# Feed-forward LayerNorm: ScalarE normalises, scale and shift are applied per partition behind the transpose

## The chip, the cores and the metric

One core of one Trainium2 chip runs the kernel as a single launch. The metric is the device time of that launch in microseconds (us), the median of several runs. All times of this document come from runs of these kernels and from one profiled execution of each.

## What is computed

A decoder trunk of two post-norm residual layers on one sequence of 256 tokens with 2048 channels, all in float32. What matters here is the LayerNorm that stands between a layer's mixer and its feed-forward part:

```python
for layer in range(2):
    mix = even_mixer(...) if layer % 2 == 0 else odd_mixer(...)
    x = layer_norm(ALPHA * x + mix, mix_ln_g[layer], mix_ln_b[layer])
    hid = jnp.square(jax.nn.relu(x @ ffn_w1[layer]))            # 2048 -> 8192
    x = layer_norm(ALPHA * x + hid @ ffn_w2[layer], ffn_ln_g[layer], ffn_ln_b[layer])

def layer_norm(x, g, b):       # mean and variance over the 2048 channels of a token
    return (x - mean) * rsqrt(var + EPS) * g + b
```

## The kernel before

The residual `xres` lies with tokens on partitions: two token blocks `tb` of 128 tokens, each with 2048 channels, handled in four chunks `n` of 512. A matrix product needs the activations the other way round, channels on partitions. So a normalised chunk goes through TensorE as four 128x128 transposes into one PSUM tile `tp` (`transpose4`, L219), of which there are two in turn. ScalarE then copies `tp` into the high part `actAh` (L213), and VectorE writes the rest, `tp` minus the high part, into `actAl` (L214). Weights are split in the same way, `wh` by ScalarE (L191) and `wl` by VectorE (L192). Every product is three matmuls: high by high, high by the weight's rest, the rest by high (L870 to L872).

The program is a list of units. A unit is six matmuls: one weight tile of two 128-channel blocks, for one token block. `at(u, f)` hangs a task in front of unit u, and the tasks of a unit are issued in the order in which they were hung, each onto its engine. Every engine runs its own instructions strictly in that order and waits on counters that the other engines raise; the framework puts in the waits.

Around a LayerNorm the units are ordered so that token block 0 ends six units ahead of token block 1, and the next stage starts with token block 0. With the last product of a token block, `z_add` adds the accumulator to `xres` and takes statistics (`bns`), `ln_stats` makes mean and reciprocal deviation (ScalarE's square root `lnsd`, L558, then three small VectorE operations ending in `lny`), `ln_apply` normalises a chunk on VectorE in two operations (L573: minus mean, times `gB`; L578: times `lny`, plus `bB`), and `ln_t` transposes and splits it. `gB` and `bB` hold scale and shift copied to all 128 partitions. In the stretch of a LayerNorm, weights are not split ahead (`hold`), unless a tile is due within four units: two are, in the second half.

Four LayerNorms are made so: ahead of the feed-forward part of layer 0 (unit group `F0u00`, about 333 us) and of layer 1 (`F1u00`, about 1441 us), ahead of layer 1's mixer (`Dk0`, about 1051 us), and, without transposes, at the end. The change is to the first two. Behind them the first product of the feed-forward part goes through `relu2` (ScalarE: relu of `acc` into `rl`, L608, then its square, L609) and is transposed four units after that product's end (`relu2_t`, rows named `tp<-ident,rl`).

Of the kernel before, what the change touches and what calls it, by code (L numbers as in the profile page):

```python
# [10 lines left out]
FT = mybir.dt.float32  # L11
# [18 lines left out]
SKEW = 6  # L30
HOLD = 4
LAND, EACH, FIRST = 3, 1.3, -1
FILL = 352
MAGIC = float(0x5F3759DF - 0x00400000)

LAG = dict(gl=7, eq=4, ek=5,
# [32 lines left out]
def trunk_kernel(ctx, tc, a, out):  # L69
# [71 lines left out]
    def at(u, f, *args):  # L141
        tasks.setdefault(u, []).append((f, args))
# [369 lines left out]

    at(start["EO00"] + 6, open_res)

    def open_ffn(g, b, u):
        st = ExitStack()
        p = st.enter_context(tc.tile_pool(name="ffnp", bufs=1, side="left"))
        fstack["s"], fstack["p"] = st, p
        load_gb(g, b, u)

    def load_gb(g, b, u):
        p = fstack["p"]
        box["g"] = p.tile([128, D], FT, name="gB")
        box["b"] = p.tile([128, D], FT, name="bB")
        for n in range(4):
            for k, (name, t) in enumerate(((g, box["g"]), (b, box["b"]))):
                src = a[name]
                at(u + 4 * n + 2 * k, SY.dma_start, t[:, n * 512:(n + 1) * 512],
                   bass.AP(tensor=src.tensor, offset=src.offset + n * 512, ap=[[0, 128], [1, 512]]))

    def conv_close():
        cstack.close()
        open_extra()
        open_ffn("mg0", "mb0", conv_done + 1)

    at(conv_done + 1, conv_close)

# [42 lines left out]
    def ln_t(tb, n):  # L580
        tp = transpose4(res["x"][:, tb, n * 512:(n + 1) * 512])
        to_act("A", slice(4 * n, 4 * n + 4), tp.rearrange("p (c t) -> p c t", t=128),
               slice(tb * 128, (tb + 1) * 128))

    def ln_out(tb, n):
        SY.dma_start(out[tb * 128:(tb + 1) * 128, n * 512:(n + 1) * 512], res["x"][:, tb, n * 512:(n + 1) * 512])

    def layer_norm(tb, u, nxt, final=False):
        at(u + 1, ln_stats, tb)
        if final:  # L590
            at(u + 2, ln_gain, tb, 0)
            for n in range(4):
                if n < 3:
                    at(u + 2, ln_gain, tb, n + 1)
                at(u + 2, ln_shift, tb, n)
                at(u + 2, ln_out, tb, n)
            return
        if tb == 0:
            at(u - 1, warm, AF.Sqrt)
            hold.update(range(u, when[nxt, 6, 1]))  # L600
        for n in range(4):
            need = when[nxt, 2 * n, tb]
            at(u + 1 + n, ln_apply, tb, n)
            at(max(u + 2 + n, min(u + 4 + 2 * n, need - 1)), ln_t, tb, n)

    def relu2(acc, tb):
        r = fstack["p"].tile([128, 512], FT, name="rl", bufs=3)
# [226 lines left out]
    def close_odd():  # L834
        odd["s"].close()
        open_extra()
        open_ffn("mg1", "mb1", start["DO0"] + 6)

    at(start["DO0"] + 6, close_odd)
    for n in range(4):  # L840
# [130 lines left out]
```

## Time and profile before

| what | value |
|---|---|
| median of 3 runs | 2177.4 us (2175.76 to 2177.59) |
| the profiled execution's own time | 2176.42 us |
| its span, first to last instruction | 2174.6 us |
| TensorE (PE) busy | 2154.5 us, 99% of the span |
| VectorE (DVE) busy | 1273.2 us, 59% |
| ScalarE (ACT) busy | 1009.6 us, 46% |
| mean granted TensorE clock | 0.998 of full |

The share of busy time is a mean over the whole program. What a change in one stage is worth is read from that stage: which engine waits there, and for what.

### The profile page before, as it was taken

To read this page: it belongs to the slowest core of one execution; us is meant where nothing else is said; L and a number is where in the kernel's file an instruction comes from. 1 tells how busy PE (TensorE), PEld (TensorE's weight loads), DVE (VectorE), ACT (ScalarE), POOL (GpSimd) and SP (SyncE) were. 2 spreads that over 40 slices of the span, in tenths; PEclk is the share of its full clock that TensorE was granted. 3 is DMA by queue.
4 is the path that set the end of the run, shared out by engine and by line. 5 is a ranking of instruction groups with operands and counts; after the bars stand their busy time and mean duration, and the time that the engine had idled before them with its cause. 6 is when DMAs were issued, how large, how long until landed. Compare 5 with 4: busy or idle time off the path is not lost.

```text
span 2174.6 us, 25528 instructions
## 1 busy us (share of the span) xinstructions
PE 2154.5 (99%) x9742; PEld 1775.7 (82%) x9742; DVE 1273.2 (59%) x1586; ACT 1009.6 (46%) x1184; POOL 0.2 (0%) x4
## 2 busy tenths in 40 slices
PE   8999999999999999999999999999999999999997
PEld 7888887888888888888887888888888888888886
DVE  6998787654445454445656456666554454454454
ACT  5445554643543543453354444436434434534541
POOL 0000000000000000000000000000000000000000
PEclk9999999999999999999999999999999999999999
DMA  7755574756555555555365545737556555555551
GB/s 256 223 193 170 184 255 140 257 187 227 189 192 194 186 187 194 190 183 194 96 202 174 185 157 192 265 102 254 193 193 228 187 193 189 182 195 189 186 191 59
DMA packets 118651, 413.83 MB, mean 190 GB/s; under 512 B 13181, under 2 KB 14973, under 8 KB 118529
## 3 DMA queue, kind: packets, MB, share of 16 engines
q1 hardware_dynamic: 118528, 412.20, 57.8%
q8 instruction: 76, 1.25, 0.2%
q14 instruction: 47, 0.38, 0.0%
HBM read 410.05 MB, written 2.10 MB: 190 GB/s over the span
## 4 chain that ended last, share of the span: by engine, by line
PE 91%; DVE 5%; ACT 1%; DMA 1%; issue 1%; SPq 0%; DVEq 0%; ACTq 0%
PE acc L870 29%; PE acc L872 29%; PE acc L871 29%; PE tp L219 2%; DVE wl L192 1%; DVE xres L573 1%; DVE xres L578 1%; ACT wh L191 1%; DMA raw<-in_w 0%; DVE actAl L214 0%; DMA raw<-in_we_out 0%; DVE bns L549 0%; DVE xres L543 0%; DMA raw<-in_we_in 0%; DVE cv L335 0%
## 5 line engine op out<-in xcount | busy, mean ns | idle before, releaser
L192 DVE TENSOR_TENSOR wl<-raw,wh 128x1024 fp32r<-128x1024 f32 (+1 forms) x753 | 918.0, 1222 | 801.9 <-ACT wh L191 800.9
L191 ACT ACTIVATE wh<-raw 128x1024 fp32r<-128x1024 f32 (+1 forms) x753 | 794.5, 1058 | 907.5 <-PE acc L872 811.2
L870 PE MATMUL acc<-wh,actAh 128*128 128x512 f32 x1728 | 688.3, 398 | 5.8 <-ACT wh L191 5.8
L872 PE MATMUL acc<-wh,actAl 128*128 128x512 f32 x1728 | 675.5, 391 | 0.0
L871 PE MATMUL acc<-wl,actAh 128*128 128x512 f32 x1728 | 674.7, 390 | 0.0
L870 PE MATMUL acc<-wh,actBh 128*128 128x512 f32 x1280 | 501.3, 392 | 0.0
L872 PE MATMUL acc<-wh,actBl 128*128 128x512 f32 x1280 | 498.4, 389 | 0.0
L871 PE MATMUL acc<-wl,actBh 128*128 128x512 f32 x1280 | 498.1, 389 | 0.0
L870 PEld LDWEIGHTS acc<-wh,actAh 128*128 128x128 f32 x1728 | 325.3, 188 | 72.7 <-ACT wh L191 6.5
L872 PEld LDWEIGHTS acc<-wh,actAl 128*128 128x128 f32 x1728 | 324.8, 188 | 68.8
L871 PEld LDWEIGHTS acc<-wl,actAh 128*128 128x128 f32 x1728 | 325.3, 188 | 67.3 <-issue 1.9
L872 PEld LDWEIGHTS acc<-wh,actBl 128*128 128x128 f32 x1280 | 240.2, 188 | 50.4
L871 PEld LDWEIGHTS acc<-wl,actBh 128*128 128x128 f32 x1280 | 240.4, 188 | 49.2
L870 PEld LDWEIGHTS acc<-wh,actBh 128*128 128x128 f32 x1280 | 240.3, 188 | 48.7
L335 DVE SCALAR_TENSOR_TENSOR cv<-hT,cpar,cv 128x256 f32<-128x256 f32 x240 | 102.0, 474 | 0.0
L213 ACT ACTIVATE actBh<-tp 128x512 fp32r<-128x512 f32 x72 | 43.1, 599 | 44.9 <-PE tp L219 44.9
L214 DVE TENSOR_TENSOR actBl<-tp,actBh 128x512 fp32r<-128x512 f32 x72 | 49.5, 688 | 15.1 <-ACT actBh L213 15.1
L545 DVE TENSOR_TENSOR xres<-xres,acc 128x512 f32<-128x512 f32 x56 | 36.7, 680 | 25.4 <-PE acc L872 25.4
L608 ACT ACTIVATE rl<-acc 128x512 f32<-128x512 f32 x64 | 38.2, 597 | 14.2 <-PE acc L872 11.6
L609 ACT ACTIVATE rl<-rl 128x512 f32<-128x512 f32 x64 | 40.5, 632 | 2.0
L219 PEld LDWEIGHTS tp<-ident,rl 128*128 128x128 f32 x256 | 32.0, 141 | 8.3
L219 PE MATMUL tp<-ident,rl 128*128 128x128 f32 x256 | 38.4, 272 | 0.0
(153 smaller groups left out, 482.5 us busy)
## 6 DMA issues: line engine op xcount, KB each, us to landing
raw<-in_w SPq DMA_DIRECT2D x512, 512.0 KB, 3.5
raw<-in_wo_in SPq DMA_DIRECT2D x96, 512.0 KB, 3.5
raw<-in_we_in SPq DMA_DIRECT2D x79, 512.0 KB, 3.6
raw<-in_we_out SPq DMA_DIRECT2D x32, 512.0 KB, 3.7
raw<-in_wo_out SPq DMA_DIRECT2D x32, 512.0 KB, 4.3
xres<-in_xres SPq DMA_DIRECT2D x8, 256.0 KB, 6.1
gB<-in_mg SPq DMA_DIRECT2D x8, 256.0 KB, 6.0
bB<-in_mb SPq DMA_DIRECT2D x8, 256.0 KB, 6.7
```

The source lines that it names most:

```text
L191: A.activation(h[:, c], r[:, c], AF.Copy)
L192: V.tensor_tensor(l[:, c], r[:, c], h.bitcast(FT)[:, c], op=OP.subtract)
L213: A.activation(h[:, kt, cols], tp, AF.Copy)
L214: V.tensor_tensor(l[:, kt, cols], tp, h.bitcast(FT)[:, kt, cols], op=OP.subtract)
L219: PE.transpose(tp[:, i * 128:(i + 1) * 128], src[:, i * 128:(i + 1) * 128], ident)
L335: V.scalar_tensor_tensor(cv[:, ct, :], hT[:, ct, k:k + T], w, cv[:, ct, :], op0=OP.mult, op1=OP.add)
L545: V.tensor_tensor(c, c, acc, op=OP.add)
L608: A.activation(r, acc, AF.Relu)
L609: A.activation(r, r, AF.Square)
L870: PE.matmul(acc, h[:, kt, c], wh[:, w], start=s0, stop=False)
L871: PE.matmul(acc, h[:, kt, c], wl[:, w], start=False, stop=False)
L872: PE.matmul(acc, l[:, kt, c], wh[:, w], start=False, stop=s1)
```

## The change

`ln_apply` and `ln_t` stay for the LayerNorm ahead of `Dk0`. Ahead of the feed-forward parts three functions take their place. `ln_norm` normalises a chunk on ScalarE in one operation, without scale and shift: its scale is `lny` and its bias is `lnm`, which one more small VectorE operation in `ln_stats` makes as minus mean times `lny`. `ln_norm_t` transposes the chunk and applies scale and shift behind the transpose, where a channel is a partition and so its scale and shift are one number per partition (`gbc`, loaded by one more DMA). Since a `tp` tile holds four blocks of channels, that is four ScalarE operations of 128 columns into `actAh` and four VectorE operations of 128 columns into a new tile `yt`, and then one subtraction into `actAl`. `ln_residual` brings scale and shift into `xres` later, with two VectorE operations for each chunk, from unit 44 of the feed-forward part on. `FILL`, a tile that nothing uses, shrinks by as much as the new small tiles take, so that what lies behind it stays where it was.

```diff
-FILL = 352
+FILL = 288
...
+        if cols:
+            box["gc"] = stat.tile([128, 2, KT], FT, name="gbc", bufs=1)
+            at(u, SY.dma_start, box["gc"], a[cols])
...
+        m = stat.tile([128, 1], FT, name="lnm")
+        V.scalar_tensor_tensor(m, mv[:, 0:1], -1.0, y, op0=OP.mult, op1=OP.mult)
+        box["shift", tb] = m
...
+    def ln_norm(tb, n):
+        c = res["x"][:, tb, n * 512:(n + 1) * 512]
+        A.activation(c, c, AF.Identity, scale=box["rstd", tb], bias=box["shift", tb])
+
+    def ln_norm_t(tb, n):
+
+        tp = transpose4(res["x"][:, tb, n * 512:(n + 1) * 512])
+        h, l = act["A"]
+        k, cols, gc = slice(4 * n, 4 * n + 4), slice(tb * 128, (tb + 1) * 128), box["gc"]
+        y = fstack["p"].tile([128, 4, 128], FT, name="yt")
+        for i in range(4):
+            s = tp[:, i * 128:(i + 1) * 128]
+            A.activation(h[:, 4 * n + i, cols], s, AF.Identity, scale=gc[:, 0, 4 * n + i:4 * n + i + 1],
+                         bias=gc[:, 1, 4 * n + i:4 * n + i + 1])
+            V.tensor_scalar(y[:, i, :], s, gc[:, 0, 4 * n + i:4 * n + i + 1], gc[:, 1, 4 * n + i:4 * n + i + 1],
+                            op0=OP.mult, op1=OP.add)
+        V.tensor_tensor(l[:, k, cols], y, h.bitcast(FT)[:, k, cols], op=OP.subtract)
+
+    def ln_residual(tb, n):
+
+        s = slice(n * 512, (n + 1) * 512)
+        c = res["x"][:, tb, s]
+        V.tensor_tensor(c, c, box["g"][:, s], op=OP.mult)
+        V.tensor_tensor(c, c, box["b"][:, s], op=OP.add)
...
-            at(u + 1 + n, ln_apply, tb, n)
-            at(max(u + 2 + n, min(u + 4 + 2 * n, need - 1)), ln_t, tb, n)
+            if nxt[0] == "F":
+                at(u + 1 + n, ln_norm, tb, n)
+                at(max(u + 2 + n, min(u + 4 + 2 * n, need - 1)), ln_norm_t, tb, n)
+                at(start[nxt] + 44 + 4 * (4 * tb + n), ln_residual, tb, n)
+            else:
+                at(u + 1 + n, ln_apply, tb, n)
+                at(max(u + 2 + n, min(u + 4 + 2 * n, need - 1)), ln_t, tb, n)
```

In the rows below the words in brackets name the counter that an instruction waits for: that of PE, of DVE or of ACT ("Activation"). ScalarE before, ahead of `F0u00`, from the first token block's square root to the first forced weight split:

```order
L558 ACTIVATE lnsd<-mv,eps 128x1 [waits DVE_49]
L213 ACTIVATE actAh<-tp 128x4x128 [waits PE_49] x2
L558 ACTIVATE lnsd<-mv,eps 128x1 [waits DVE_49]
L213 ACTIVATE actAh<-tp 128x4x128 [waits PE_49] x3
L191 ACTIVATE wh<-raw 128x1024 [waits DMAHW5_49,Activation_49]
```

ScalarE now, from the first square root to the third chunk:

```order
L561 ACTIVATE lnsd<-mv,eps 128x1 [waits DVE_49]
L593 ACTIVATE xres<-xres,lnm,lny 128x512 [waits DVE_49]
L593 ACTIVATE xres<-xres,lnm,lny 128x512 x2
L603 ACTIVATE actAh<-tp,gbc 128x128 [waits PE_49]
L603 ACTIVATE actAh<-tp,gbc 128x128 [waits DVE_49] x3
L593 ACTIVATE xres<-xres,lnm,lny 128x512
L603 ACTIVATE actAh<-tp,gbc 128x128 [waits PE_49]
L603 ACTIVATE actAh<-tp,gbc 128x128 [waits DVE_49] x3
L561 ACTIVATE lnsd<-mv,eps 128x1 [waits DVE_49]
L593 ACTIVATE xres<-xres,lnm,lny 128x512 [waits DVE_49]
L603 ACTIVATE actAh<-tp,gbc 128x128 [waits PE_49]
L603 ACTIVATE actAh<-tp,gbc 128x128 [waits DVE_49] x3
```

Before, a chunk is one ScalarE instruction that waits for PE. Now it is one to normalise, and four behind the transpose, of which the last three each wait for VectorE. The second square root, which stood behind two copies, stands behind two whole chunks.

VectorE before, at the same place, from the first token block's last normalisation to the second block's statistics:

```order
L573 SCALAR_TENSOR_TENSOR xres<-xres,mv,gB 128x512 [waits DMAHW2_49]
L578 SCALAR_TENSOR_TENSOR xres<-xres,lny,bB 128x512 [waits DMAHW4_49,DVE_49]
L545 TENSOR_TENSOR xres<-xres,acc 128x512 [waits PE_49]
L549 BN_STATS bns<-xres 128x6 [waits DVE_49]
L214 TENSOR_TENSOR actAl<-tp,actAh 128x4x128 [waits Activation_49]
L573 SCALAR_TENSOR_TENSOR xres<-xres,mv,gB 128x512 [waits DMAHW6_49]
L578 SCALAR_TENSOR_TENSOR xres<-xres,lny,bB 128x512 [waits DMAHW0_49,DVE_49]
L214 TENSOR_TENSOR actAl<-tp,actAh 128x4x128 [waits Activation_49]
L545 TENSOR_TENSOR xres<-xres,acc 128x512 [waits PE_49]
L549 BN_STATS bns<-xres 128x6 [waits DVE_49]
L557 BN_AGGR mv<-bns 128x2 [waits DVE_49]
```

VectorE now, from the new small operation to the second block's statistics:

```order
L567 SCALAR_TENSOR_TENSOR lnm<-mv,lny 128x1 [waits DVE_49]
L548 TENSOR_TENSOR xres<-xres,acc 128x512 [waits PE_49]
L552 BN_STATS bns<-xres 128x6 [waits DVE_49]
L605 TENSOR_SCALAR yt<-tp,gbc 128x128 [waits Activation_49] x4
L607 TENSOR_TENSOR actAl<-yt,actAh 128x4x128 [waits DVE_49]
L605 TENSOR_SCALAR yt<-tp,gbc 128x128 [waits DVE_49,Activation_49]
L605 TENSOR_SCALAR yt<-tp,gbc 128x128 [waits Activation_49] x3
L607 TENSOR_TENSOR actAl<-yt,actAh 128x4x128 [waits DVE_49]
L548 TENSOR_TENSOR xres<-xres,acc 128x512 [waits PE_49]
L552 BN_STATS bns<-xres 128x6 [waits DVE_49]
L560 BN_AGGR mv<-bns 128x2 [waits DVE_49]
```

The two normalising operations of each chunk are gone from VectorE. In front of each subtraction stand four operations on `tp`, each of which waits for ScalarE. The second block's statistics still stand behind the first two chunks.

## Rows read from the trace of the kernel before

**Rows 1.** The page, busy time by engine, share of the span.

```profile
PE 2154.5 (99%) x9742; PEld 1775.7 (82%) x9742; DVE 1273.2 (59%) x1586; ACT 1009.6 (46%) x1184; POOL 0.2 (0%) x4
```

**Rows 2.** Stretches around both LayerNorms: length, busy us (count) by engine, clock, DMA.

```profile
325.00:365.00 40.00, 37.94 (x183) 30.73 (x182) 32.02 (x51) 13.97 (x21) 0.00 (x0) 1.00 0.36 117
1430.00:1470.00 40.00, 39.77 (x192) 32.32 (x191) 25.92 (x43) 11.88 (x18) 0.00 (x0) 1.00 0.20 65
```

**Rows 3.** Timeline of PE, layer 0, fifth transposes: start, us, [idle before].

```profile
346.85 0.66 PE L219 MATMUL tp<-ident,xres 128*128 128x128 f32 x4 [1.24 <-DVE actAl L214]
```

**Rows 4.** Timeline of PE: layer 1's last transposes, first of `rl`, both layers.

```profile
1460.11 0.60 PE L219 MATMUL tp<-ident,xres 128*128 128x128 f32 x4
1463.32 0.60 PE L219 MATMUL tp<-ident,xres 128*128 128x128 f32 x4
1469.25 0.60 PE L219 MATMUL tp<-ident,rl 128*128 128x128 f32 x4
...
362.75 0.60 PE L219 MATMUL tp<-ident,rl 128*128 128x128 f32 x4
```

**Rows 5.** Timelines of ACT and DVE around the square roots.

```profile
332.90 0.29 ACT L558 ACTIVATE lnsd<-mv,eps 128x1 f32<-128x1 f32 x1 [2.93 <-DVE mv L557]
...
1440.72 0.29 ACT L558 ACTIVATE lnsd<-mv,eps 128x1 f32<-128x1 f32 x1 [7.55 <-DVE mv L557]
1450.31 0.30 ACT L558 ACTIVATE lnsd<-mv,eps 128x1 f32<-128x1 f32 x1 [2.63 <-DVE mv L557]
...
1441.04 0.16 DVE L560 RECIPROCAL lny<-lnsd 128x1 f32<-128x1 f32 x1 [0.17 <-ACT lnsd L558]
1441.57 0.75 DVE L573 SCALAR_TENSOR_TENSOR xres<-xres,mv,gB 128x512 f32<-128x512 f32 x1
1448.57 0.68 DVE L543 SCALAR_TENSOR_TENSOR xres<-xres,acc 128x512 f32<-128x512 f32 x1
```

**Rows 6.** Groups of ACT by shape: count, busy us, mean ns, idle before.

```profile
L191 ACT ACTIVATE wh<-raw 128x1024 fp32r<-128x1024 f32 x751 | 793.3, 1059 | 904.7 <-PE acc L872 811.2 <-DMA raw<-in_w 30.6 <-DVE cv L335 17.6
L469 ACT ACTIVATE PT<-tp 128x128 f32<-128x128 f32 x8 | 2.2, 280 | 0.0
L360 ACT ACTIVATE c<-cv 128x256 f32<-128x256 f32 x8 | 2.9, 418 | 3.9 <-DVE cv L358 3.9
L385 ACT ACTIVATE c<-c,cpar 128x256 f32<-128x256 f32 x8 | 4.7, 591 | 4.1 <-DVE c L380 4.0
L609 ACT ACTIVATE rl<-rl 128x512 f32<-128x512 f32 x64 | 40.5, 632 | 2.0
```

**Rows 7.** Groups of DVE by shape.

```profile
L578 DVE SCALAR_TENSOR_TENSOR xres<-xres,lny,bB 128x512 f32<-128x512 f32 x32 | 23.8, 750 | 0.8
L214 DVE TENSOR_TENSOR actAl<-tp,actAh 128x512 fp32r<-128x512 f32 x24 | 16.2, 684 | 6.8 <-ACT actAh L213 6.8
L452 DVE CUSTOM_DVE_ANT_0 P<-sd,bias 128x128 f32<-128x128 f32 x8 | 2.3, 287 | 0.9 <-DMA bias<-in_abias 0.8
L332 DVE TENSOR_SCALAR cv<-hT,cpar 128x256 f32<-128x256 f32 x8 | 2.9, 402 | 0.0
L229 DVE TENSOR_SCALAR cyi<-cnh 128x256 int32<-128x256 int32 x1 | 0.3, 294 | 0.0
L192 DVE TENSOR_TENSOR wl<-raw,wh 128x1024 fp32r<-128x1024 f32 x751 | 916.6, 1224 | 799.0 <-ACT wh L191 797.9
```

**Rows 8.** Timeline of ACT in layer 1's mixer: two operations with one pointer operand.

```profile
1117.25 0.51 ACT L715 ACTIVATE wd<-wd,aT 128x256 f32<-128x256 f32 x1 [1.67 <-DVE wd L714]
1117.67 0.39 ACT L716 ACTIVATE wd<-wd,aT 128x128 f32<-128x128 f32 x1
```

**Rows 9.** Clock behind the last matmul (windows); two matmuls at the start (timeline).

```profile
2163.40:2168.00 4.60, 0.00 (x0) 0.00 (x0) 4.25 (x11) 0.29 (x1) 0.00 (x0) 0.78 0.31 114
...
9.46 0.63 PE L870 MATMUL acc<-wh,actAh 128*128 128x512 f32 x1
9.88 0.63 PE L871 MATMUL acc<-wl,actAh 128*128 128x512 f32 x1
```

More of the change, by code (lines that the diff above doesn't have):

```diff
@@ L513, in trunk_kernel, with open_ffn @@
     at(start["EO00"] + 6, open_res)
-    def open_ffn(g, b, u):
+    def open_ffn(g, b, u, cols):
         st = ExitStack()
@@ L518, in open_ffn, with load_gb @@
         fstack["s"], fstack["p"] = st, p
-        load_gb(g, b, u)
-    def load_gb(g, b, u):
+        load_gb(g, b, u, cols)
+    def load_gb(g, b, u, cols=None):
         p = fstack["p"]
+        if cols:
+            box["gc"] = stat.tile([128, 2, KT], FT, name="gbc", bufs=1)
+            at(u, SY.dma_start, box["gc"], a[cols])
         box["g"] = p.tile([128, D], FT, name="gB")
@@ L533, in conv_close @@
         open_extra()
-        open_ffn("mg0", "mb0", conv_done + 1)
+        open_ffn("mg0", "mb0", conv_done + 1, "mc0")
     at(conv_done + 1, conv_close)
@@ L836, in close_odd @@
         open_extra()
-        open_ffn("mg1", "mb1", start["DO0"] + 6)
+        open_ffn("mg1", "mb1", start["DO0"] + 6, "mc1")
     at(start["DO0"] + 6, close_odd)
@@ L958 @@
         arr[f"mg{n}"], arr[f"mb{n}"] = i["mix_ln_g"][n], i["mix_ln_b"][n]
+        arr[f"mc{n}"] = np.stack([i["mix_ln_g"][n], i["mix_ln_b"][n]]).reshape(2, KT, 128).transpose(2, 0, 1)
         arr[f"fg{n}"], arr[f"fb{n}"] = i["ffn_ln_g"][n], i["ffn_ln_b"][n]
```

## The prediction

> **What bounds the kernel now.** I read the page's busy times first: TensorE (PE) is busy 99% of the span, so only a stretch in which PE waits can be shortened, and any wait put before it shows at once [rows 1]. Then the stretches around the two LayerNorms that change: in 40 us, PE idles 2.06 us in layer 0 and 0.23 us in layer 1 [rows 2]. That is all the change can gain: 2.3 us. The largest piece, 1.24 us, is the fifth set of transposes, which waits for one of the two `tp` tiles to be read out by VectorE [rows 3]. So how fast ScalarE and VectorE empty `tp` is what PE meets first. PE wants a chunk every 3.21 us there (1460.11 to 1463.32) [rows 4].
>
> The mark by which I measure the stretch is the first transpose of `rl`: it comes behind all eight chunks on ScalarE's queue and then the relu. From the first square root `lnsd` to it are 28.53 us in layer 1 (1440.72 to 1469.25) and 29.85 us in layer 0 (332.90 to 362.75) [rows 4, 5].
>
> **The change part by part.** Call N a chunk's normalisation on ScalarE, and P its readout from `tp`. Removed from VectorE are two operations of 0.75 us for each chunk [rows 7]. Added are these:
>
> *The readout goes step by step.* The order shows that VectorE's k-th operation on `tp` waits for ScalarE, and ScalarE's next one waits for VectorE. All four blocks lie in one PSUM tile, and the two engines take turns on it: a step is one ScalarE operation, a hand-over, one VectorE operation, a hand-over. Nothing of this sequence overlaps.
> - ScalarE, 128 columns from PSUM without a pointer operand: 0.28 us (L469) [rows 6]. Scale and bias are now one number per partition, read by pointer. At 256 columns an operation has 0.418 us without a pointer (L360), 0.51 with one (L715), 0.591 with two (L385) [rows 6, 8]: two cost 0.17. So 0.45.
> - VectorE, 128 columns from PSUM: 0.287 us (L452); two pointers cost 0.402 (L332) less 0.294 (L229), 0.11 [rows 7]. So 0.39: 0.28 is the bound from below; L332's whole 0.40, at twice the columns, is about as much.
> - A hand-over: square root 1440.72 + 0.29 = 1441.01, VectorE's reciprocal at 1441.04: 0.03 [rows 5].
>
> A step is 0.45 + 0.39 + 0.06 = 0.90 us, four are 3.60, and P without the last hand-over is 3.57. Bounds of a step: 0.28 + 0.29 + 0.06 = 0.63 if pointers were free, and 0.59 + 0.40 + 0.06 = 1.05 if 128 columns cost what the 256 of L385 and L332 cost. Where PE's pace leaves 3.21, P takes 3.57, and VectorE's subtraction (0.68, L214 [rows 7]) comes on top.
>
> The Trainium skill, "ScalarE: Activation LUTs", section "What ACT_TABLE_LOAD costs", gives 186 ns plus 0.833 ns per column, and 93 ns for each pointer operand. The rows here say 0.08 to 0.09 a pointer; by the page the operation is an estimated 0.48 us, and the result would be 1.9 us later.
>
> *N on ScalarE.* 512 columns in SBUF have 0.632 us (L609) [rows 6]; with two pointers 0.80. A successor starts 0.09 before the end (L716 at 1117.67, L715 ending 1117.76) [rows 8], so 0.71 apart. One small operation (`lnm`) joins the chain: the first normalisation began 0.85 us after `lnsd` (1441.57) [rows 5]; with the rest of `lny` and `lnm` I take 1.2.
>
> *The walk*, in us from the first `lnsd`:
> 1. N of chunks 0 to 2 from 1.2; ScalarE is free for P0 at 3.3, which ends at 6.9; subtraction, VectorE free at 7.5.
> 2. ScalarE does N3 and begins P1 at 7.1; VectorE joins at 7.6; P1 ends at 10.7, VectorE is free at 11.3.
> 3. Only then comes the second token block's last `z_add`. From it to its `lnsd` 1.74 us passed (1448.57 to 1450.31) [rows 5]: `lnsd` at 13.0, where it stood at 9.6.
> 4. On ScalarE P2 stands behind that `lnsd` and N of the fifth chunk: 13.0 + 1.2 + 0.71 = 15.0; ends at 18.5. The fifth transposes need P2's tile, as they did before, so PE stands until 18.6.
> 5. Two N, then P3 from 19.4 to 23.0; subtraction to 23.6; P4 to 26.7, its subtraction to 27.3.
> 6. A forced weight split (1.06 on ScalarE, L191, then 1.22 on VectorE, L192 [rows 6, 7]) stands ahead of P5, one ahead of P6. VectorE: split to 29.2, P5 and subtraction to 32.9, split to 34.1, P6 and subtraction to 37.8, P7 to 40.9. PE has the fifth's buffer and late weight tiles to wait for again on the way; all of it lies inside.
> 7. ScalarE ends P7 at 40.5, then relu and square, at most 2 x 0.632 [rows 6]: the transposes of `rl` at 41.8.
>
> So the mark moves by 41.8 - 28.5 = 13.3 us in layer 1 and by 41.8 - 29.9 = 11.9 in layer 0. Behind it the stages are the old ones, and PE has nothing to catch up with.
>
> *The rest costs nothing.* `ln_residual` puts 16 VectorE operations of about 0.7 us into a layer's middle, one pair every four units, where VectorE is busy 59% [rows 1]; without that cover it would be 11 us a layer. The first sum that needs `xres` again comes after unit 72, the last pair. `gbc` is one more small DMA on SP's queue, ahead of the first `gB`; in the time until its use at P0, eight loads of 256 KB pass behind it. `gB` and `bB` are needed later than before. `FILL` moves no address.
>
> **Sum.** The profiled execution's own time is 2176.4 us, 1.0 under the median. 2176.4 + 13.3 + 11.9 = 2201.6, so about 2202 us, 1.1% slower. The bounds: a step of 0.63, with N at 0.63, walked in the same way, puts the mark at 33.5, +5.0 and +3.6: 2185. A step of 1.05 adds 8 x 4 x 0.15 = 4.8 to each LayerNorm: 2211.
>
> **The rivals.**
> *Not slower: the readouts lie side by side.* If the waits were always already met, ScalarE would need 0.71 + 4 x 0.36 = 2.15 us a chunk and VectorE 4 x 0.31 + 0.6 = 1.84, both under PE's 3.21 [rows 4]; PE would lose part of its 2.3 us of waits: 2174 to 2176. It decides at a step of about (3.21 - 0.6) / 4 = 0.65. The waits in the order speak against it, since each step's wait is for the instruction just issued on the other engine; only the free-pointer bound of 0.63 comes near, and step 3 stands even then. Chance 4%.
>
> The Trainium skill, "PSUM — Partial Sum Buffer", section "PSUM bank collisions raise a hardware error", has two engines collide on one bank even where both only read, and the compiler put a dependency between them. By that rule the turns can't be left out. No run here shows a collision.
>
> *Pointers cost little on these operations.* Then a step is near 0.63 and the time near 2186. L385 and L332 are other functions at other widths, which is what speaks for it; three ACT rows in line speak against. Chance 13%.
>
> *PE's clock falls in the long waits and costs extra.* PE stands about six us in step 4. At the program's end PE has nothing to do from 2163.4 on, and the granted clock's mean over the next 4.6 us is 0.78: full for some 2.6 us, then half, 1.2 GHz [rows 9]. At the program's start matmuls come 0.42 us apart (9.46 to 9.88) [rows 9]; twelve of them and a chunk's transposes in 3.21 us [rows 4] leave under 0.27 each at full speed, so a slow one loses about 0.2. Between step 4 and the mark PE has under 16 us of work in a stretch of 23, so one fall is hidden; it costs if the clock is still low behind the mark, some 3.5 us a layer if 16 matmuls are slow: 2209. The Trainium skill, "TensorE: Matmul & The Clock Gate", part 1, has the clock halved after idling; the trace agrees at the end, where the mean of 0.78 shows it. Chance 10%.
>
> **How the numbers follow.** Forecast 73%, the three rivals 4, 13 and 10%. The range runs from just above the lower bound to the upper: 2187 to 2212. About 0.2%, 4.4 us, is what a measurement here can tell from no change. Faster needs the first rival and more than its whole gain: 2%. Same: the rest of it and a pointer-free step with less behind it: 5%. Slower: 93%.
>
> **What would show it.** Right: in the timeline ScalarE's and VectorE's 128-column operations alternate, one step every 0.9 us, and VectorE's idle time is put down to ScalarE's line; PE's longest new wait, about 6 us, is at the fifth transposes; the stretch from the first `lnsd` to the transposes of `rl` is near 42 us in both layers; the LayerNorm ahead of `Dk0` and the end are unchanged. Wrong: a step under 0.65 us; a mark that moves by less than 6 us; PE idle elsewhere, as behind late weights after the mark; or a clock at half for many us behind it.

## The result, and the profile after

The changed kernel takes 2209.34 us (median of 4 runs, 2208.18 to 2210.14) where the kernel before took 2177.03 beside it: 1.0147 times as long, 95% interval 1.0135 to 1.0160. The profiled execution has 2209.19 us, a span of 2207.4 and a mean clock of 0.994.

PE has as many instructions as before; its share of the span is one point lower, although its busy time is 10.1 us longer [rows 1]:

```profile
PE 2164.6 (98%) x9742; PEld 1780.2 (81%) x9742; DVE 1299.0 (59%) x1658; ACT 1039.1 (47%) x1248; POOL 0.2 (0%) x4
```

The first chunk behind the transpose, in layer 0. First ScalarE's timeline, then VectorE's (start, us, instruction, idle time before it and what ended it):

```profile
337.15 0.44 ACT L603 ACTIVATE actAh<-tp,gbc 128x128 fp32r<-128x128 f32 x1
338.07 0.46 ACT L603 ACTIVATE actAh<-tp,gbc 128x128 fp32r<-128x128 f32 x1 [0.48 <-DVE yt L605]
339.01 0.46 ACT L603 ACTIVATE actAh<-tp,gbc 128x128 fp32r<-128x128 f32 x1 [0.48 <-DVE yt L605]
```

```profile
337.63 0.41 DVE L605 TENSOR_SCALAR yt<-tp,gbc 128x128 f32<-128x128 f32 x1 [1.32 <-ACT actAh L603]
338.56 0.41 DVE L605 TENSOR_SCALAR yt<-tp,gbc 128x128 f32<-128x128 f32 x1 [0.53 <-ACT actAh L603]
339.50 0.41 DVE L605 TENSOR_SCALAR yt<-tp,gbc 128x128 f32<-128x128 f32 x1 [0.53 <-ACT actAh L603]
```

Read the two together: ScalarE 338.07 to 338.53, VectorE 338.56 to 338.97, ScalarE 339.01. While one works the other stands, and the idle time of each is put down to the other. A step is 339.01 - 338.07 = 0.94 us.

What PE waits for, over the whole program, the three largest groups that the kernel before does not have (total us, times, longest):

```profile
PE tp L219 <- DVE yt L605: 11.9, 4, 5.6
PE tp L219 <- ACT rl L645: 4.8, 2, 2.4
PE acc L908 <- DVE actAl L607: 4.4, 4, 1.7
```

PE's timeline at the fifth transposes [rows 3] and at the mark [rows 4], layer 0 and then layer 1, and ScalarE's first square root of each [rows 5]:

```profile
352.94 1.12 PE L219 MATMUL tp<-ident,xres 128*128 128x128 f32 x4 [5.60 <-DVE yt L605]
376.94 0.66 PE L219 MATMUL tp<-ident,rl 128*128 128x128 f32 x4 [2.38 <-ACT rl L645]
1476.02 1.12 PE L219 MATMUL tp<-ident,xres 128*128 128x128 f32 x4 [5.61 <-DVE yt L605]
1500.02 0.66 PE L219 MATMUL tp<-ident,rl 128*128 128x128 f32 x4 [2.39 <-ACT rl L645]
```

```profile
333.85 0.30 ACT L561 ACTIVATE lnsd<-mv,eps 128x1 f32<-128x1 f32 x1 [2.93 <-DVE mv L560]
1456.92 0.29 ACT L561 ACTIVATE lnsd<-mv,eps 128x1 f32<-128x1 f32 x1 [7.55 <-DVE mv L560]
```

So from `lnsd` to the mark it is 43.09 us in layer 0 and 43.10 in layer 1, 13.24 and 14.57 more than before. From the mark to the next LayerNorm's first `lnsd` it is 689.41 and 689.43 us, where before it was 687.74 both times: 1.67 and 1.69 more. These are the next `lnsd`, before and then after:

```profile
1050.49 0.29 ACT L558 ACTIVATE lnsd<-mv,eps 128x1 f32<-128x1 f32 x1 [8.85 <-DVE mv L557]
2156.99 0.29 ACT L558 ACTIVATE lnsd<-mv,eps 128x1 f32<-128x1 f32 x1 [25.17 <-DVE mv L557]
```

```profile
1066.35 0.30 ACT L561 ACTIVATE lnsd<-mv,eps 128x1 f32<-128x1 f32 x1 [8.85 <-DVE mv L560]
2189.45 0.30 ACT L561 ACTIVATE lnsd<-mv,eps 128x1 f32<-128x1 f32 x1 [25.17 <-DVE mv L560]
```

The remaining 1.63 us of the span's 32.8 lie ahead of layer 0's first `lnsd` (0.95), between `Dk0` and `F1u00` (0.34) and at the end (0.34).

The clock, from the table of stretches (length, busy us and count of PE, PEld, DVE, ACT, POOL, then granted clock and DMA):

```profile
350.00:355.00 5.00, 2.06 (x7) 1.87 (x8) 2.40 (x6) 3.45 (x7) 0.00 (x0) 0.55 0.00 0
375.00:380.00 5.00, 3.06 (x11) 2.55 (x12) 3.17 (x5) 3.13 (x6) 0.00 (x0) 0.78 0.01 3
380.00:385.00 5.00, 5.00 (x21) 4.03 (x20) 2.45 (x2) 3.61 (x5) 0.00 (x0) 0.87 0.62 204
```

It is low around the wait of 5.60 us and again behind the mark and its wait of 2.38 us, where matmuls come 0.43 us apart from 377.93 to 380.92, against 0.23 later (382.47, 382.70).

### The profile page after: what moved, and what is told of

The parts are those of the page before. It is cut to its first block, busy times and chain, and to the rows that moved or that the text cites. A ratio compares the mean times of both kernels' runs of the same rounds, so it can differ in the third digit from the quotient of the medians.

```text
span 2207.4 us, 25672 instructions
## 1 busy us (share of the span) xinstructions
PE 2164.6 (98%) x9742; PEld 1780.2 (81%) x9742; DVE 1299.0 (59%) x1658; ACT 1039.1 (47%) x1248; POOL 0.2 (0%) x4
## 4 chain that ended last, share of the span: by engine, by line
PE 89%; DVE 5%; ACT 3%; DMA 2%; issue 1%; SPq 0%; DVEq 0%; ACTq 0%
PE acc L908 28%; PE acc L906 28%; PE acc L907 28%; PE tp L219 2%; DVE yt L605 1%; ACT actAh L603 1%; DVE wl L192 1%; ACT wh L191 1%; DMA raw<-in_w 0%; ACT xres L593 0%; DVE xres L579 0%; DVE xres L584 0%; DMA raw<-in_we_out 0%; DMA raw<-in_xt 0%; DVE bns L552 0%
## 5 line engine op out<-in xcount | busy, mean ns | idle before, releaser
L213 ACT ACTIVATE actBh<-tp 128x512 fp32r<-128x512 f32 x72 | 43.1, 598 | 40.9 <-PE tp L219 40.9
L548 DVE TENSOR_TENSOR xres<-xres,acc 128x512 f32<-128x512 f32 x56 | 36.7, 679 | 25.2 <-PE acc L908 25.2
L605 DVE TENSOR_SCALAR yt<-tp,gbc 128x128 f32<-128x128 f32 x64 | 26.2, 410 | 33.7 <-ACT actAh L603 33.0
L603 ACT ACTIVATE actAh<-tp,gbc 128x128 fp32r<-128x128 f32 x64 | 28.7, 455 | 30.4 <-DVE yt L605 30.4
```

Source lines behind the costliest of these rows:

```text
L213: A.activation(h[:, kt, cols], tp, AF.Copy)
L603: A.activation(h[:, 4 * n + i, cols], s, AF.Identity, scale=gc[:, 0, 4 * n + i:4 * n + i + 1], bias=gc[:, 1, 4 * n + i:4 * n + i + 1])
L605: V.tensor_scalar(y[:, i, :], s, gc[:, 0, 4 * n + i:4 * n + i + 1], gc[:, 1, 4 * n + i:4 * n + i + 1], op0=OP.mult, op1=OP.add)
```

## The experiments

The theory: the turns that ScalarE and VectorE take on one `tp` tile make the stretch long, and the other parts of the change are nearly free. The rivals: many small operations with pointers cost it in any order; the normalisation on ScalarE costs it; the clock costs it. All diffs are against the changed kernel, except where another is named. Each ratio is to the kernel before as it ran beside that run (2177.03, 2177.09 or 2177.57 us).

| kernel | us | ratio to before, 95% interval | `lnsd` to mark, layers 0 and 1 |
|---|---|---|---|
| before | 2177.03 | | 29.85, 28.53 |
| changed | 2209.34 | 1.0135 to 1.0160 | 43.09, 43.10 |
| e1, reads in two blocks | 2187.31 | 1.0028 to 1.0064 | 34.34, 34.42 |
| e2, VectorE alone reads | 2184.17 | 1.0021 to 1.0046 | 32.28, 32.28 |
| e3, turns, no pointers | 2188.83 | 1.0041 to 1.0073 | 34.63, 34.63 |
| e4, changed, PE kept busy | 2205.16 | 1.0115 to 1.0147 | 43.07, 43.07 |
| e5, ScalarE alone reads | 2178.14 | 0.9996 to 1.0013 | 29.37, 29.42 |
| e6, e5 with later normalisation | 2176.36 | 0.9988 to 1.0005 | 28.34, 28.39 |
| e7, VectorE normalises, turns | 2207.09 | 1.0123 to 1.0155 | 42.76, 42.52 |
| e8, ScalarE normalises, old readout | 2181.02 | 1.0008 to 1.0026 | 31.35, 30.24 |
| e9, changed, later normalisation | 2205.33 | 1.0112 to 1.0143 | 41.78, 41.76 |
| e10, e1 with later normalisation | 2180.96 | 1.0005 to 1.0024 | 30.22, 30.31 |
| e11, e1, PE kept busy | 2184.44 | 1.0020 to 1.0045 | 31.98, 33.35 |
| e12, two tiles | 2181.64 | 1.0011 to 1.0029 | 31.32, 31.36 |

**e1: the same operations in two blocks.**

```diff
         for i in range(4):
-            s = tp[:, i * 128:(i + 1) * 128]
-            A.activation(h[:, 4 * n + i, cols], s, AF.Identity, scale=gc[:, 0, 4 * n + i:4 * n + i + 1],
-                         bias=gc[:, 1, 4 * n + i:4 * n + i + 1])
-            V.tensor_scalar(y[:, i, :], s, gc[:, 0, 4 * n + i:4 * n + i + 1], gc[:, 1, 4 * n + i:4 * n + i + 1],
-                            op0=OP.mult, op1=OP.add)
+            A.activation(h[:, 4 * n + i, cols], tp[:, i * 128:(i + 1) * 128], AF.Identity,
+                         scale=gc[:, 0, 4 * n + i:4 * n + i + 1], bias=gc[:, 1, 4 * n + i:4 * n + i + 1])
+        for i in range(4):
+            V.tensor_scalar(y[:, i, :], tp[:, i * 128:(i + 1) * 128], gc[:, 0, 4 * n + i:4 * n + i + 1],
+                            gc[:, 1, 4 * n + i:4 * n + i + 1], op0=OP.mult, op1=OP.add)
```

> Only the order of the reads changes: ScalarE's four blocks of tp first, then VectorE's four, so that a chunk has one hand-over from ScalarE to VectorE instead of eight in turn. The operations, their number, their pointers and the subtraction stay. Theory (the turns cost the time): ScalarE is through with a chunk after about 1.6 to 1.8 us, VectorE after another 1.6; no VectorE operation waits for an operation of ScalarE's on the same chunk but the first; ScalarE does the next chunk's normalisation meanwhile. PE's longest wait falls from 5.6 us to 3 or less, the stretch from the first lnsd to the transposes of rl from 43.1 to 30 to 34 us, the time to 2177 to 2186. Rival (many small operations with pointers cost it, in whatever order): VectorE's and ScalarE's work per chunk is as before, the stretch stays at 40 us or more and the time at 2203 to 2210.

22.0 us of the change's 32.3 are gone, with every operation and pointer in place. So it is the turns, and small operations with pointers in any order are out as the main cause. ScalarE's and VectorE's timeline of the third chunk:

```profile
346.76 1.48 ACT L602 ACTIVATE actAh<-tp,gbc 128x128 fp32r<-128x128 f32 x4
```

```profile
348.28 1.36 DVE L605 TENSOR_SCALAR yt<-tp,gbc 128x128 f32<-128x128 f32 x4 [2.27 <-ACT actAh L602]
```

Four in a row take 1.48 and 1.36 us; in turn, four steps of 0.94 take 3.75. But VectorE still waits until ScalarE's last read, and all three numbers ended above what was expected: PE's longest wait (3.83 us, not 3 or less), the stretch (34.3 and 34.4, not 30 to 34) and the time (by 1.3 us). PE's timeline and the stretch behind it show why:

```profile
349.79 1.09 PE L219 MATMUL tp<-ident,xres 128*128 128x128 f32 x4 [3.83 <-DVE yt L605]
```

```profile
350.00:355.00 5.00, 5.00 (x15) 4.03 (x15) 4.12 (x11) 4.08 (x9) 0.00 (x0) 0.50 0.00 0
355.00:360.00 5.00, 5.00 (x26) 4.13 (x25) 3.62 (x8) 2.94 (x7) 0.00 (x0) 0.95 0.32 105
```

Behind a wait of 3.83 us the granted clock is 0.50 (1.2 GHz) for 5 us, and PE gets 15 instructions done where the next 5 us hold 26. e10 and e11 follow this up.

**e2: VectorE alone reads `tp`.**

```diff
-            A.activation(h[:, 4 * n + i, cols], s, AF.Identity, scale=gc[:, 0, 4 * n + i:4 * n + i + 1],
-                         bias=gc[:, 1, 4 * n + i:4 * n + i + 1])
-            V.tensor_scalar(y[:, i, :], s, gc[:, 0, 4 * n + i:4 * n + i + 1], gc[:, 1, 4 * n + i:4 * n + i + 1],
-                            op0=OP.mult, op1=OP.add)
+            V.tensor_scalar(y[:, i, :], tp[:, i * 128:(i + 1) * 128], gc[:, 0, 4 * n + i:4 * n + i + 1],
+                            gc[:, 1, 4 * n + i:4 * n + i + 1], op0=OP.mult, op1=OP.add)
+        A.activation(h[:, k, cols], y, AF.Copy)
```

> Only VectorE reads tp: its four operations write yt as before, and ScalarE copies yt, 512 columns in SBUF, to actAh in one operation; normalisation on ScalarE, the pointers on VectorE and the subtraction stay. Theory (two engines in turn on one PSUM tile cost the time): tp is empty after 4 x 0.41 = 1.6 us, a chunk takes VectorE 1.6, a wait for the copy of 0.7, and 0.7 for the subtraction, about 3.0 us against PE's 3.2; PE's waits are 2 us or less each, the stretch is 29 to 32 us, and the time 2175 to 2181. Rival (the normalisation ahead of ScalarE's part and the pointer operations on VectorE are what make it late): the wait of 5.6 us stays above 4, and the time at 2195 or more.

The wait for VectorE's readout, 5.6 us before, is 0.6 at most, as the theory has it, but the time is 3 us above its upper end and the stretch 0.3. The expectation filled VectorE with 3.0 us a chunk against PE's 3.2 and left no room for the two `wl` splits (1.2 us each) and the `z_add` that stand between the chunks. PE now waits in many small places (groups of waits, total, times, longest):

```profile
PE acc L905 <- DVE wl L192: 2.5, 5, 0.7
PE acc L904 <- ACT actAh L604: 2.2, 2, 1.1
PE tp L219 <- DVE yt L602: 1.2, 2, 0.6
```

**e3: the turns without pointers.**

```diff
-            A.activation(h[:, 4 * n + i, cols], s, AF.Identity, scale=gc[:, 0, 4 * n + i:4 * n + i + 1],
-                         bias=gc[:, 1, 4 * n + i:4 * n + i + 1])
-            V.tensor_scalar(y[:, i, :], s, gc[:, 0, 4 * n + i:4 * n + i + 1], gc[:, 1, 4 * n + i:4 * n + i + 1],
-                            op0=OP.mult, op1=OP.add)
+            A.activation(h[:, 4 * n + i, cols], s, AF.Identity, scale=1.0, bias=0.0)
+            V.tensor_scalar(y[:, i, :], s, 1.0, 0.0, op0=OP.mult, op1=OP.add)
```

> The turns stay, but both readouts of tp take scale 1 and shift 0 as numbers in the instruction, in place of the pointers (left out: scale and shift of the channels at the feed-forward inputs). It measures what the pointers cost. Theory (a step is the sum of both operations and two hand-overs, and pointers cost 0.17 and 0.11 us): a step of about 0.65 us instead of 0.94, a chunk 2.6 instead of 3.75, the stretch about 33 to 35 us, the time 2185 to 2191. Rival (the pointers cost nothing, an operation is set by its tile and the turn): a step of 0.9 or more, time 2206 to 2210. Other rival (only the number of turns counts, through a hand-over that is much longer than the 0.03 us): step between 0.8 and 0.9, time 2198 to 2205.

Step, stretch and time are as the theory had them. ScalarE's timeline, same chunk:

```profile
338.93 0.28 ACT L603 ACTIVATE actAh<-tp 128x128 fp32r<-128x128 f32 x1 [0.36 <-DVE yt L604]
339.56 0.28 ACT L603 ACTIVATE actAh<-tp 128x128 fp32r<-128x128 f32 x1 [0.36 <-DVE yt L604]
```

A step is 0.63 us, the sum's bound from below, and the time of 2188.8 is 4 us above the 2185 that the prediction worked out for it. So two pointers cost 0.18 us on ScalarE (0.455 less 0.274, means) and 0.12 on VectorE (0.410 less 0.291). The groups of instructions (count, busy us, mean ns, idle before), the changed kernel over the whole program and then e3 from 330 to 380 us:

```profile
L603 ACT ACTIVATE actAh<-tp,gbc 128x128 fp32r<-128x128 f32 x64 | 28.7, 455 | 30.4 <-DVE yt L605 30.4
L605 DVE TENSOR_SCALAR yt<-tp,gbc 128x128 f32<-128x128 f32 x64 | 26.2, 410 | 33.7 <-ACT actAh L603 33.0
```

```profile
L603 ACT ACTIVATE actAh<-tp 128x128 fp32r<-128x128 f32 x32 | 8.5, 274 | 12.7 <-DVE yt L604 12.7
L604 DVE TENSOR_SCALAR yt<-tp 128x128 f32<-128x128 f32 x32 | 9.3, 291 | 11.3 <-ACT actAh L603 10.9
```

They cost 20.5 us of time only because the turns put every operation on the path: e1 carries the same pointers and is no slower. In the profiles 16.9 us of it lie in the two stretches and 3.3 behind the marks, where e4 will show the clock's part.

**e4: PE kept busy in its two waits.** (The added matmuls have 512 columns, not the 256 that the expectation names, and come 0.23 to 0.24 us apart.)

```diff
+    def keep_warm(k):
+        p = psum.tile([128, 512], FT, name="sd")
+        h = act["B"][0]
+        for i in range(k):
+            PE.matmul(p, h[:, 0, 0:128], h[:, 0:2, :].rearrange("p k t -> p (k t)"), start=i == 0, stop=i == k - 1)
...
+        if (tb, n) == (1, 0):
+            keep_warm(23)
...
+                    if (c, n, tb) == (0, 0, 0):
+                        at(u + 4, keep_warm, 9)
```

> The changed kernel with 23 more matmuls of 256 columns on PE ahead of the fifth chunk's transposes and 9 ahead of the first transposes of rl, whose sums nobody reads: PE works where it stood for 5.6 and 2.4 us, and nothing else changes. It asks whether the clock that is low behind the mark is PE's own idling, and what it costs. Theory (PE's waits lower its clock, and the matmuls behind the mark are slow for it): the granted clock stays at 1.00 in both stretches, the stretch from lnsd to rl stays at 43.1 us, the 1.7 us a layer behind it go: 2205 to 2207 us, 1.5 to 4 us less than the changed kernel. Rival (the low clock costs nothing, the 1.7 us behind the mark are something else): 2208 to 2211. Other rival (the added matmuls delay PE more than they give back): over 2211.

The clock stays up, and the time is 4.2 us lower, within the expected 2205 to 2207 (stretches around the fifth transposes and behind the mark):

```profile
350.00:355.00 5.00, 4.63 (x22) 3.34 (x21) 2.45 (x6) 3.41 (x7) 0.00 (x0) 1.00 0.00 0
375.00:380.00 5.00, 4.67 (x23) 3.63 (x22) 3.60 (x4) 3.97 (x5) 0.00 (x0) 1.00 0.20 51
```

The mark stays at 43.07, and from it to the next `lnsd` it is 687.80 and 687.79 us again. So the 1.7 us a layer behind the mark are the clock's (the two profiled spans differ by 4.5 us: 3.3 lie behind the marks, and 1.2 ahead of the first `lnsd`, 332.64 us against 333.85, where the two kernels do not differ), and the low clock behind the wait of 5.6 us costs nothing: the mark is where it was. The Trainium skill, "TensorE: Matmul & The Clock Gate", part 1, has the clock halved after idling; the trace agrees, with 0.50 behind e1's wait of 3.83 us and 1.00 here, where the waits were filled.

**e5 and e6: ScalarE alone reads `tp`; then the normalisations of block 1 one unit later as well.**

```diff
-        y = fstack["p"].tile([128, 4, 128], FT, name="yt")
+        y = fstack["p"].tile([128, 4, 128], FT, name="yt", bufs=2)
         for i in range(4):
-            s = tp[:, i * 128:(i + 1) * 128]
-            A.activation(h[:, 4 * n + i, cols], s, AF.Identity, scale=gc[:, 0, 4 * n + i:4 * n + i + 1],
-                         bias=gc[:, 1, 4 * n + i:4 * n + i + 1])
-            V.tensor_scalar(y[:, i, :], s, gc[:, 0, 4 * n + i:4 * n + i + 1], gc[:, 1, 4 * n + i:4 * n + i + 1],
-                            op0=OP.mult, op1=OP.add)
+            A.activation(y[:, i, :], tp[:, i * 128:(i + 1) * 128], AF.Identity, scale=gc[:, 0, 4 * n + i:4 * n + i + 1],
+                         bias=gc[:, 1, 4 * n + i:4 * n + i + 1])
+        V.tensor_copy(h[:, k, cols], y)
```

and in e6 also:

```diff
-                at(u + 1 + n, ln_norm, tb, n)
+                at(u + 1 + n + tb, ln_norm, tb, n)
```

> Only ScalarE reads tp: its four operations with pointers write yt (two buffers of it), and VectorE makes actAh from yt with one copy of 512 columns and then the subtraction; the rest as in the changed kernel. Theory (two engines in turn on tp cost the time): a chunk takes ScalarE 0.71 + 4 x 0.36 = 2.2 us and VectorE about 1.4, both under PE's 3.2; the second token block's lnsd comes 10 to 10.7 us after the first, as before the change; PE's one wait of note is that of the fifth transposes, 2 to 3.5 us, since ScalarE reads the third chunk only behind that lnsd and one normalisation; the stretch from lnsd to the transposes of rl is 29.5 to 32.5 us and the time 2176 to 2182. Rival (ScalarE's queue is the limit, whoever else reads): stretch above 34 us, time above 2186.

> The kernel in which ScalarE alone reads tp, and the second token block's four normalisations one unit later, so that on ScalarE the readout of the third chunk stands straight behind the second lnsd and not behind a normalisation that waits for lny and lnm. Theory (the fifth transposes wait for that readout): the wait is 1.2 to 2 us shorter than with the normalisation ahead, the stretch 0.5 to 2 us shorter in each layer, the time 2174 to 2179. Rival (the place of the normalisation does not matter, or a later one makes a later set of transposes wait as long): within 1 us of the kernel without the move, or slower.

Both times came out as the theory had them, the waits and e5's stretch lower: e5 waits 1.41 us and not 2 to 3.5, its stretch is 29.4 and not 29.5 or more, and e6 takes 0.99 us off the wait and not 1.2 or more. PE's timeline at the fifth transposes, e5 and then e6:

```profile
347.35 0.66 PE L219 MATMUL tp<-ident,xres 128*128 128x128 f32 x4 [1.41 <-ACT yt L602]
```

```profile
346.69 0.66 PE L219 MATMUL tp<-ident,xres 128*128 128x128 f32 x4 [0.42 <-ACT xres L593]
```

What e6 adds is the order on ScalarE: with the third chunk's readout straight behind the second `lnsd`, the wait falls from 1.41 to 0.42 us, which is now for a normalisation, and the stretch falls by 1.0 us in both layers. e6 is 33.0 us faster than the changed kernel; from the kernel before it can't be told apart, since its stretches are only 1.5 and 0.1 us shorter than those of before.

**e7 and e8: one part of the change each.** e7 keeps the readout in turns and normalises on VectorE; e8 normalises on ScalarE, applies `gB` and `bB` in two VectorE operations before the transposes, and reads `tp` out as before.

```diff
-        A.activation(c, c, AF.Identity, scale=box["rstd", tb], bias=box["shift", tb])
+        V.tensor_scalar(c, c, box["rstd", tb], box["shift", tb], op0=OP.mult, op1=OP.add)
```

and e8:

```diff
+    def ln_norm_gb(tb, n):
+        ln_norm(tb, n)
+        ln_residual(tb, n)
...
-                at(u + 1 + n, ln_norm, tb, n)
-                at(max(u + 2 + n, min(u + 4 + 2 * n, need - 1)), ln_norm_t, tb, n)
-                at(start[nxt] + 44 + 4 * (4 * tb + n), ln_residual, tb, n)
+                at(u + 1 + n, ln_norm_gb, tb, n)
+                at(max(u + 2 + n, min(u + 4 + 2 * n, need - 1)), ln_t, tb, n)
```

> The changed kernel with its normalisation on VectorE (one operation of 512 columns for a chunk) in place of ScalarE; the readout in turns stays. Theory (the readout in turns costs the time, and ScalarE's normalisation lies beside VectorE's subtraction): on VectorE it lies beside nothing, so up to 0.7 us a chunk comes on top: the stretch is 44 to 49 us and the time 2210 to 2222. Rival (the normalisation on ScalarE makes ScalarE late and costs a good part of the 32 us): the stretch falls below 40 us and the time below 2203.

> The other part alone: the normalisation on ScalarE as in the changed kernel, but scale and shift right behind it on VectorE, two operations of 0.69 us on 512 columns of xres, and then the transposes and the readout of before (ScalarE copies tp in one operation, VectorE subtracts). Theory (only the readout of tp costs): VectorE has the work of before, the chain from lnsd to a chunk is some 1 us longer, PE waits 1 to 3 us in a stretch: 28.5 to 32 us from lnsd to rl, time 2175 to 2181. Rival (the normalisation on ScalarE and the longer chain cost it): stretch of 35 us or more, time above 2188.

With ScalarE's normalisation taken out, the change still costs 30.0 us (e7); with it and the old readout, 3.9 (e8). So the normalisation on ScalarE is out as the cause. But in e7 the extra time that the theory expected did not come. VectorE normalises a chunk in 0.54 us, not 0.7 (groups of instructions, one stretch of layer 0: count, busy us, mean ns):

```profile
L593 DVE TENSOR_SCALAR xres<-xres,lny,lnm 128x512 f32<-128x512 f32 x8 | 4.1, 543 | 0.1
```

and three of them take 1.46 where ScalarE's three took 2.23, so the first readout begins 2.77 us behind `lnsd` and not 3.30. In which engine the normalisation lies is worth 0.3 to 0.6 us a layer. e8 lies at the upper end of its expected time. In it PE's two longest waits in the stretches, 1.9 us for `actAl` and 1.2 for `xres`, both stand ahead of transposes.

**e9: the order on ScalarE in the changed kernel.**

```diff
-                at(u + 1 + n, ln_norm, tb, n)
+                at(u + 1 + n + tb, ln_norm, tb, n)
```

> The changed kernel with the second token block's four normalisations one unit later, so that on ScalarE the third chunk's readout stands straight behind the second lnsd; the turns stay. It asks what the wait of step 4 is worth. Theory (PE's wait of 5.6 us is lnsd, the wait for lny and lnm, one normalisation and then 3.6 us of turns): the wait is 3.4 to 4.2 us, the stretch from lnsd to the transposes of rl 1 to 2 us shorter than 43.1, the time 2204 to 2207. Rival (behind it the sum of the turns sets the mark whatever the order): the wait is shorter, but the stretch is within 0.5 us and the time 2208 to 2210.

The stretch is 1.3 us shorter in both layers, within the expected 1 to 2. The wait fell only to 4.54 us, not to 3.4 to 4.2: now the normalisation comes behind the readout, and the fifth transposes wait for it. PE's timeline:

```profile
351.91 1.05 PE L219 MATMUL tp<-ident,xres 128*128 128x128 f32 x4 [4.54 <-ACT xres L593]
```

**e10 and e11: what keeps e1 above the kernel before.** e10 is e1 with the line of e9; e11 is e1 with e4's `keep_warm` ahead of the fifth transposes alone:

```diff
     def ln_norm_t(tb, n):
+        if (tb, n) == (1, 0):
+            keep_warm(8)
```

> The kernel with ScalarE's four reads of tp ahead of VectorE's four, and the second token block's normalisations one unit later. Theory (the wait of 3.8 us at the fifth transposes, and the clock that falls in it, are what keeps that kernel 10 us above the one of before): the wait falls to 1.6 to 2.5 us, the granted clock stays at 1.00 in 350 to 355 us, the stretch falls from 34.3 to 30 to 32 us, the time to 2177 to 2182. Rival (the single hand-over for each chunk, in which VectorE stands while ScalarE reads, keeps VectorE late): 2185 or more.

> The kernel with ScalarE's four reads of tp ahead of VectorE's four, and 8 matmuls of 512 columns (0.39 us each, sums read by nobody) on PE ahead of the fifth transposes. In that kernel the granted clock is 0.50 from 350 to 355 us, behind a wait of 3.8 us. Theory (PE is the bound there, so a clock at half for 5 us costs 2 to 2.5 us a layer): the clock stays at 1.00, the stretch falls from 34.3 to 31.8 to 32.5 us, the time to 2182 to 2184. Rival (PE would have waited for the next chunks anyway, as in the changed kernel, where 15 us at low clock cost only 1.7): 2186 to 2188.

With the later normalisation the wait is 2.15 us, the clock stays up (first row below, e10; e1 had 0.50), and the time falls by 6.4 us to where the theory had it. (The two stretches fall by 8.2; against that, e10's profile has a wait of 0.9 us for `stg` in layer 1's mixer that e1's has not.) In e11 the eight matmuls come 0.24 us apart and not 0.39; they fill 2.09 us, and 1.99 us of the wait are left. In layer 0 the clock stayed at 1.00 (second row) and the stretch fell by 2.4 us to 31.98, as the theory had it. In layer 1, behind the same matmuls and the same wait, it did not (third row), the stretch is 1.4 us longer than that of layer 0, and the time of 2184.4 lies just above the expected 2184. So of e1's 10.3 us above the kernel before, about 3 are the clock's: e11 is 2.9 us faster, and its two stretches together are 3.4 us shorter, with the clock still low for a part in layer 1:

```profile
350.00:355.00 5.00, 5.00 (x25) 3.85 (x24) 4.82 (x11) 5.00 (x12) 0.00 (x0) 1.00 0.00 0
```

```profile
350.00:355.00 5.00, 5.00 (x26) 3.98 (x24) 4.12 (x11) 5.00 (x13) 0.00 (x0) 1.00 0.00 0
1460.00:1465.00 5.00, 5.00 (x19) 3.94 (x20) 4.12 (x11) 4.26 (x10) 0.00 (x0) 0.66 0.01 3
```

**e12: the written order of the changed kernel, but a tile for each reader.**

```diff
         tp = transpose4(res["x"][:, tb, n * 512:(n + 1) * 512])
+        tq = psum.tile([128, 512], FT, name="sd")
+        for i in range(4):
+            PE.transpose(tq[:, i * 128:(i + 1) * 128], res["x"][:, tb, n * 512 + i * 128:n * 512 + (i + 1) * 128], ident)
...
-            V.tensor_scalar(y[:, i, :], s, gc[:, 0, 4 * n + i:4 * n + i + 1], gc[:, 1, 4 * n + i:4 * n + i + 1],
+            V.tensor_scalar(y[:, i, :], tq[:, i * 128:(i + 1) * 128], gc[:, 0, 4 * n + i:4 * n + i + 1], gc[:, 1, 4 * n + i:4 * n + i + 1],
```

> The changed kernel, but PE transposes each chunk twice, into two PSUM tiles: ScalarE reads its four blocks from the one, VectorE from the other, in the written order of the changed kernel. Theory (the turns belong to the one tile that both read, not to the engines or the operations): no VectorE operation on a tile waits for ScalarE's; both read side by side, 0.36 and 0.34 us apart; PE has four more transposes of 0.6 us in all for each of 16 chunks, 9.6 us, and waits 2 to 3 us at the fifth transposes: stretch 35 to 38 us, time 2187 to 2193. Rival (two engines that read PSUM at once, or that alternate in writing actAh and yt, hold each other up in any case): a step stays near 0.9 us and the time at 2208 or more.

The turns are gone. ScalarE's and VectorE's timeline of the second chunk: both start as soon as PE lets them, and run beside each other from 339.76 to 340.83.

```profile
339.32 1.51 ACT L606 ACTIVATE actAh<-tp,gbc 128x128 fp32r<-128x128 f32 x4 [0.88 <-PE tp L219]
```

```profile
339.76 1.37 DVE L608 TENSOR_SCALAR yt<-sd,gbc 128x128 f32<-128x128 f32 x4 [1.29 <-PE sd L600]
```

So the operations, or two engines reading PSUM, do not make the turns. It takes both the shared tile and the alternating order: e12 changes the tile, e1 the order, and either ends them. The Trainium skill, "PSUM — Partial Sum Buffer", section "PSUM bank collisions raise a hardware error", has the compiler order two engines on one bank, readers too; the trace agrees so far, as the waits are gone once the tiles are two; no run here shows a collision. The time came out 5 us below the expected range: four more transposes cost PE 0.40 to 0.43 us a chunk (the second set starts 0.43 us behind the first, 338.69 to 339.12; the next chunk's starts at 342.30, 3.61 us behind and not 3.21), 6.4 to 6.9 us in all and not 9.6, and they cover the expected wait, for no wait at `tp` longer than 0.4 us is left in the stretches.

## Why the prediction was right, and where its sum was short

The forecast was 2202 us in a range of 2187 to 2212; 2209.3 lies in it, 7 us above. By its own steps:

- **The readout goes step by step.** Right, and shown: turns in the trace, gone in e12 by a second tile, gone for the most part in e1 by order alone. The step was mis-sized: 0.94 us, not 0.90 (ScalarE 0.455, VectorE 0.41 where 0.39 was taken, hand-overs 0.03 and 0.04). Over eight chunks of four steps, 0.037 us a step make 1.2 us a LayerNorm.
  By the Trainium skill's "ScalarE: Activation LUTs", section "What ACT_TABLE_LOAD costs", the ScalarE operation would have been an estimated 0.48 us; the trace's 0.455 lies at the sum's own value.
- **The walk.** Its steps are found in layer 0, in us from `lnsd`: the first readout begins at 3.3 (predicted 3.3), the second `lnsd` is at 13.45 (13.0), the third readout begins at 15.3 (15.0), the fifth transposes start at 19.1 (18.6) behind a wait of 5.60 us (about 6), the fourth readout begins at 19.9 (19.4), the mark is at 43.1 (41.8). The lag grows with the number of steps done, 8 at the second `lnsd`, 12 at the fourth readout and 32 at the mark, as a step that is 0.037 us too short makes it.
- **Pointers cost little.** As a rival it fell: with pointers the step is 0.94. Without them (e3) the time is 2188.8, where the prediction's lower bound had 2185: its walk had the mark at 33.5 us, and e3 has it at 34.6.
- **The readouts lie side by side.** In the changed kernel, no. e12 shows that with two tiles they do, and e5 and e6 that, with one reader, the rest of the change costs nothing that can be measured.
- **The clock.** The rival was held to be separate from the forecast, whose sum has nothing for it; in fact both happened. It cost 1.7 us a layer behind the mark (e4), not 3.5: about 7 matmuls were fully slow, not 16. This is the largest miss, 3.4 us.
- **The rest costs nothing.** Right for `ln_residual` and `gbc`: in e4, which has all of it, the stretch from the mark to the next `lnsd` is 687.80 us, against 687.74 before. Of the 1.63 us that remain, 0.95 lie ahead of the first `lnsd`; it stands between 332.1 and 335.0 in the profiles of this study, whose kernels hardly differ up to there, so 0.95 is within what executions differ by. But the LayerNorm ahead of `Dk0` and the one at the end are not unchanged, as the prediction has them, and the change is not confined to two LayerNorms: `ln_stats` now makes `lnm` in all four, twice in each, and only two of them use it. It is one more operation of 0.16 us behind `lny`, and in the other two the normalisation begins 0.19 us later behind the square root. At `Dk0` PE's wait ahead of the first transposes is 0.44 us where it was 0.24. So about 0.2 of the 0.34 us at each of the two places is its price; where the rest comes from stays open. The group in the changed kernel, then PE's timeline at `Dk0`, before and after:

```profile
L567 DVE SCALAR_TENSOR_TENSOR lnm<-mv,lny 128x1 f32<-128x1 f32 x8 | 1.3, 159 | 0.3
```

```profile
1053.03 0.63 PE L219 MATMUL tp<-ident,xres 128*128 128x128 f32 x4 [0.24 <-DVE xres L578]
1069.08 0.63 PE L219 MATMUL tp<-ident,xres 128*128 128x128 f32 x4 [0.44 <-DVE xres L584]
```

Sum of the misses: 25.2 predicted, plus 2.6 for the step and the walk, plus 3.4 for the clock, plus 1.6 elsewhere, is 32.8, the difference of the two spans.

What stays open: whether VectorE and ScalarE could read different blocks of one tile at the same time without the waits was not tried, since they would then have to be unordered on one tile. Why the clock fell in one layer of e11 and not in the other is open too.

## What to carry to other kernels

Two engines that read one PSUM tile alternately pay the sum of their operations, hand-overs and pointers included; either write one engine's reads as a block, or give the tile to one reader, or give each reader a tile. Count a readout per tile against the pace at which the producer wants the tile back (here 3.75 us against 3.21), and look at what stands ahead of it in its engine's queue: moving one normalisation behind the readout was worth 1.0 to 1.3 us a LayerNorm (e6, e9), and 4.1 where the shorter wait also left the clock up (e10). Behind a good order the change costs nothing, but no order tried here made it a gain. A wait of the engine that sets the pace can cost more than its length, for its clock may be low when it has work again; a wait filled with idle matmuls showed what that share is.

## What the runs showed of the hardware

- Two pointer operands cost 0.18 us on a 128-column ScalarE operation and 0.12 us on a VectorE one, both from PSUM (e3).
- VectorE applies two pointers to 512 columns in SBUF in 0.54 us (e7), less than the 0.75 of each of the two operations that it stands for, which have a second tensor [rows 7], and converts 512 columns from SBUF in 0.43 us (e5).
- The clock was 0.50 for 5 us behind a wait of 3.83 us (e1), 0.87 on the mean of 380 to 385 us behind one of 2.38 us that ended at 376.94 (the changed kernel), and 1.00 behind one of 2.15 us (e10). Behind 2.09 us of matmuls and a wait of 1.99 us it was 1.00 in one layer of e11, and 0.66 on the mean of 5 us in the other.
- A second set of four transposes right behind the first adds 0.40 to 0.43 us to PE, though its row says 0.60 (e12).
